# A float32 encoder on one core: feed-forward column groups projected in pairs, with seven products in place of eight in two block steps of each pair

## The chip, the cores and the metric

The kernel runs on one core of one Trainium2 chip. The metric is the device time of one execution in microseconds (us). Engines are named as in the profile: PE is TensorE (matmuls; PEld its weight loads), DVE is VectorE, ACT is ScalarE, POOL is GpSimd, SP is SyncE, which issues the weight loads from HBM.

## The reference

A trunk of two residual layers over 256 tokens of width 2048, in float32. The first layer mixes tokens by grouped-query attention, the second by a gated linear recurrence; each is followed by a SwiGLU feed-forward layer of inner width 5632, which is what the change touches:

```python
def swiglu(h, w_gate, w_up, w_down):
    return (jax.nn.silu(h @ w_gate) * (h @ w_up)) @ w_down

for i in range(DEPTH):
    h = rms_norm(x, norm_mix[i])
    ...
    x = x + mix
    x = x + swiglu(rms_norm(x, norm_ffn[i]), ffn_w_gate[i], ffn_w_up[i], ffn_w_down[i])
```

## The kernel before

**Numbers in two parts.** Each float32 operand is split into a rounded part `hi` and a rest `lo` (both float32r), and a product is made of three matmuls: hi x hi, hi x lo, lo x hi. Weights arrive as float32 in pieces of 512 KB, called halves here (`load_half`, L107): 128 rows by 8 x 128 numbers, in the feed-forward layers two tiles of contraction (k) by 512 columns. A load by SP fills `raw`, ScalarE casts it to `hi` (L116), VectorE makes `lo` = raw - hi (L117). Each of the three has five buffers, so a cast can begin when PE has left the half five places back.

**A projection with tokens in the rows.** `project_tokens` (L209) holds the activations' tiles as the stationary operand: 128 k by 128 tokens, for the two blocks a of the 256 tokens. It makes 512 columns at a time, in two PSUM banks, one for each token block. A half has 2 k x 2 token blocks x 3 = 12 matmuls of 512 columns.

**The feed-forward layer** (`ffn`, L634). The inner width of 44 tiles is done in three parts of 12, 16 and 16 tiles (`PARTS`). A part is made in units of 512 columns: first the gate (8 halves, 16 tiles of k), whose banks ScalarE turns into silu (`fg`), then up (8 halves), whose banks VectorE multiplies into `fu`. `turned` (L345) turns a unit so that the inner width lies on the partitions: VectorE transposes squares of 32 x 32 (`tb`), and 16 copies put them together (`tf`), every other one on ScalarE and on VectorE. The four tiles are then split into hi and lo (L645, L646). When a part is complete, `output` (L376) projects it down, four column groups of 512 one after the other, and adds each bank into the residual `x_tok` (L384). In the last part each finished column group is squared, turned and scaled for the next norm (`Norm.add`, L313; operands `xg`), while PE works on the next group. `PSUM` has two pools of four banks: `ps_a` for these projections, which take two each, and `ps_m`.

**What sets the order.** TensorE's instructions stand in the order in which the program issues them. The order of every other engine's queue is made by a scheduler at build time; on the chip each of them is worked off strictly in that order. Small pieces of work are hung on a counter of TensorE's steps (`later`, `step`). At the border between the two layers the recurrence begins with `project_two`, which takes the first 8 k tiles for two column tiles, then the other 8, and with `nr.spread`, four small matmuls that need the norm's factors.

Of the kernel before, what the change touches and what calls it, by code (L numbers as in the profile page):

```python
# [25 lines left out]
NBLK = 8  # L26
DFF = 5632
PARTS = [12, 16, 16]
HALF = 8
WIDE = 512  # L30
NCOL = D // WIDE
FOUR = WIDE // P
COMMON = {"sq", "nsq", "nr", "nrt", "rsq_s", "nj", "ndg", "nrb"}
EPS = 1e-6
LRU_C = 8.0
GRID_W = 64
# [33 lines left out]
def trunk(ctx, tc, w, out):  # L70
    nc = tc.nc
    act, dve, pool, pe, sync = nc.scalar, nc.vector, nc.gpsimd, nc.tensor, nc.sync
# [9 lines left out]
    ffn_scope = ctx.enter_context(ExitStack())  # L82
# [3 lines left out]
    def nm(s):  # L86
        uid[0] += 1
        return f"{s}_{uid[0]}"
# [14 lines left out]
        return i  # L103


    def load_half(src, n, pieces=1, then=None):
# [3 lines left out]
        newest["load"] = sync.dma_start(out=raw[:, :n, :], in_=src[:, :n, :])  # L110
        if then:
            then()
        for i in range(pieces):
            sl = slice(i * n // pieces, (i + 1) * n // pieces)
            newest["tiles"] = hi, lo
            newest["cast"] = act.copy(hi[:, sl, :], raw[:, sl, :])  # L116
            dve.tensor_tensor(lo[:, sl, :], raw[:, sl, :], hi[:, sl, :].bitcast(F32), ALU.subtract)  # L117
        return [(hi[:, i, :], lo[:, i, :]) for i in range(n)]
# [5 lines left out]
    def wide(name):  # L124
        src = w[name]
        return [(src[c, i], HALF) for c in range(src.shape[0]) for i in range(src.shape[1])]

    def ffn_order(l):
        units = [wide(f"w_gate{l}"), wide(f"w_up{l}")]
        seq, i = [], 0  # L130
        for p, n in enumerate(PARTS):
            for _ in range(n // FOUR):
                for u in units:
                    seq += u[i : i + KT // 2]
                i += KT // 2
            seq += wide(f"w_down{l}_{p}")
        return seq

    order = [(w["w_k"][i], HALF) for i in range(len(KEY_TILES))]
# [51 lines left out]
    def new_acc():  # L191
        return ps_a.tile([P, 2 * S], F32, tag="acc", name=nm("acc"))
# [18 lines left out]
    def project_tokens(xs, ready=0, close=None):  # L211
# [15 lines left out]
                step()  # L227
        return accs

    def three(o, hi, lo, x, start, stop):  # L230
        pe.matmul(o, hi, x[:, :S], start=start, stop=False)  # L231
        pe.matmul(o, hi, x[:, S:], start=False, stop=False)  # L232
        pe.matmul(o, lo, x[:, :S], start=False, stop=stop)  # L233
# [59 lines left out]


    class Norm:
        def __init__(self, gname, gofs):
            self.g = (gname, gofs)
            self.xs = []
            self.sums = tmp("nsq", (P, 2, NCOL))

# [12 lines left out]
        def add(self, c):  # L313
            for a in range(2):
                act.activation(tmp("nj", (P, WIDE), bufs=1), x_tok[:, a, c, :], AF.Square, accum_out=self.sums[:, a, c : c + 1])
            for f in turned(x_tok[:, :, c, :]):
                self.operand(f, True)


        def finish(self):  # L320
# [23 lines left out]
    def turned(src):  # L344
        b = fp[0].tile([P, 2, FOUR, P], F32, tag="tb", name=nm("tb"))  # L345
        f = fp[0].tile([P, 8, FOUR, 32], F32, tag="tf", name=nm("tf"))
        for a in range(2):
            dve.transpose(b[:, a, :, :], src[:, a, :])  # L348
        for q in range(4):
            for i in range(4):  # L350
                o, y = f[32 * i : 32 * i + 32, q::4, :, :], b[32 * q : 32 * q + 32, :, i, :]
                y = y.rearrange("p a (k t) -> p a k t", k=FOUR)
                if i % 2:
                    act.copy(o, y)  # L354
                else:
                    dve.tensor_copy(o, y)  # L356
# [19 lines left out]
    def output(xs, norm=None, end=False, ready=0, close=None):  # L376
        for c in range(NCOL):
            accs = project_tokens(xs, ready, None if c else close)
            for a, acc in enumerate(accs):
                n = 2 if end and c == NCOL - 1 else 1  # L380
                for i in range(n):
                    sl = slice(i * WIDE // n, (i + 1) * WIDE // n)
                    y = x_tok[:, a, c, sl]
                    dve.tensor_tensor(y, y, acc[:, sl], ALU.add)  # L384
                    if end:
                        sync.dma_start(out=out[:, a, c, sl], in_=y)
            if norm is not None:
                norm.add(c)
        if norm is not None:
            norm.finish()  # L390

# [8 lines left out]
    def table_act(*a, **k):  # L400
        table_op(act.activation(*a, **k))
# [226 lines left out]
        scope.pop()  # L628
        open_ffn()

    nf = Norm("norm_ffn", 0)
    output(o_t, nf, ready=KT - 2, close=end_attention)


    def ffn(norm, nxt):
        def unit():
            g, u = (fp[0].tile([P, 2, WIDE], F32, tag=t, name=nm(t), bufs=1) for t in ("fg", "fu"))
            for a, acc in enumerate(project_tokens(norm.xs)):
                table_act(g[:, a, :], acc, AF.Silu, scale=norm.rt[:, a : a + 1])
            for a, acc in enumerate(project_tokens(norm.xs)):  # L640
                dve.scalar_tensor_tensor(u[:, a, :], acc, norm.rt[:, a : a + 1], g[:, a, :], ALU.mult, ALU.mult)
            for f in turned(u):
                h = act_tile()
                hi, lo = (h[:, o : o + S].rearrange("p (q t) -> p q t", t=32) for o in (0, S))
                act.copy(hi, f)  # L645
                dve.tensor_tensor(lo, f, hi.bitcast(F32), ALU.subtract)  # L646
                yield h

        for p, n in enumerate(PARTS):
            hid = [h for _ in range(n // FOUR) for h in unit()]  # L650
            last = p == len(PARTS) - 1
            if last and nxt is not None:
                ln_exp_tables()
            output(hid, nxt if last else None, last and nxt is None)

    nr = Norm("norm_mix", KT)
    ffn(nf, nr)
# [127 lines left out]
        ln_exp_tables()  # L785
        open_ffn()

    nf = Norm("norm_ffn", KT)
    output(g_t, nf, ready=KT - 2, close=end_recurrence)
    ffn(nf, None)  # L790

# [84 lines left out]
```

## Time and profile before

| | |
|---|---|
| median of 3 runs | 2037.51 us (2037.05 to 2037.53) |
| span of the profiled execution | 2034.8 us |
| PE busy | 2021.0 us, 99% |
| DVE busy | 1311.9 us, 64% |
| ACT busy | 1157.2 us, 57% |
| read from HBM | 382.13 MB |

The span is that of one profiled execution, from the first to the last instruction; the runs' time has a little more around it. A busy engine is one with an instruction under way, and since PE's matmuls overlap, their rate is read from how many begin in a stretch, not from the length of one. In a row of a group of instructions the columns are: line, engine, operation, output<-inputs, shapes, count | busy us, mean ns of one | idle time of the engine just before them, and what ended it. In a window row: from:to, its length, busy time of PE, PEld, DVE, ACT and POOL with their counts, PE's granted clock, the share of DMA, GB/s; where PE alone was asked for, only its busy time and count stand ahead of the clock. In a timeline row: start, duration, engine, line, operation. In a row of waits: who waited for whom, us in total, times, the longest.

### The profile page before, as it was taken

How to read it: one execution, taken by the hardware profiler on the slowest of the kernel's cores; microseconds unless marked ns; L12 is line 12 of the kernel's file. 1: busy time of each engine (PE TensorE's matmuls, PEld its weight loads, DVE VectorE, ACT ScalarE, POOL GpSimd, SP SyncE). 2: the span in 40 equal slices, each digit the busy share in tenths (PEclk: the TensorE clock that was granted, in tenths of full speed). 3: DMA queues.
4: the chain of work that ended last, by engine and by line, in shares of the span. 5: the costliest groups of instructions: out<-in, count | busy, mean ns of one | idle time of the engine just before them, and what ended most of it. 6: DMA issues, size and time to landing. Idle time of an engine off the chain costs nothing.

```text
span 2034.8 us, 27445 instructions
## 1 busy us (share of the span) xinstructions
PE 2021.0 (99%) x10124; PEld 1722.5 (85%) x10124; DVE 1311.9 (64%) x1899; ACT 1157.2 (57%) x1776; POOL 168.6 (8%) x213
## 2 busy tenths in 40 slices
PE   9999999999999999999899999999999999999999
PEld 8898888888888888888799998888888888888887
DVE  7998765654665445667778987765555556555553
ACT  7665755544555345556689987755435554355442
POOL 1563000000000000000134330000000000000000
PEclk9999999999999999999999999999999999999999
DMA  8444565665666656666556555566666666666664
GB/s 319 157 135 145 186 202 193 186 203 191 187 197 197 195 195 193 186 199 196 188 165 188 187 157 194 180 205 197 190 194 195 193 190 196 196 189 195 197 202 129
DMA packets 108998, 386.02 MB, mean 190 GB/s; under 512 B 12224, under 2 KB 12992, under 8 KB 108736
## 3 DMA queue, kind: packets, MB, share of 16 engines
q1 hardware_dynamic: 108720, 384.26, 59.7%
q8 instruction: 79, 1.29, 0.3%
q14 instruction: 55, 0.45, 0.1%
q10 hardware_dynamic: 144, 0.02, 0.0%
HBM read 382.13 MB, written 2.10 MB: 189 GB/s over the span
## 4 chain that ended last, share of the span: by engine, by line
PE 54%; issue 40%; DVE 2%; DMA 2%; ACT 1%; POOL 0%; SPq 0%; DVEq 0%; POOLq 0%
PE acc L223 40%; PE acc L201 3%; PE acc L231 3%; PE acc L232 3%; PE acc L233 3%; PE pm L232 1%; PE pm L233 1%; PE pm L231 1%; DVE lo L117 1%; DMA x_tok<-in_xt_dram 1%; DMA graw<-in_w_gates_dram 0%; DMA raw<-in_w_k_dram 0%; PE pm L576 0%; DMA raw<-in_w_qv_dram 0%; ACT hi L116 0%
## 5 line engine op out<-in xcount | busy, mean ns | idle before, releaser
L117 DVE TENSOR_TENSOR lo<-raw,hi 128x1024 fp32r<-128x1024 f32 (+1 forms) x708 | 868.7, 1230 | 665.5 <-ACT hi L116 657.1
L116 ACT CAST hi<-raw 128x1024 fp32r<-128x1024 f32 (+1 forms) x708 | 739.4, 1047 | 751.7 <-PE acc L223 744.0
L223 PE MATMUL acc<-hi,xg 128*128 128x512 f32 x2816 | 867.8, 389 | 0.0
L223 PEld LDWEIGHTS acc<-hi,xg 128*128 128x128 f32 x2816 | 528.6, 188 | 109.6
L223 PE MATMUL acc<-hi,act 128*128 128x512 f32 x1920 | 594.2, 389 | 0.0
L223 PE MATMUL acc<-lo,xg 128*128 128x512 f32 x1408 | 547.7, 389 | 0.0
L223 PEld LDWEIGHTS acc<-hi,act 128*128 128x128 f32 x1920 | 360.4, 188 | 74.4
L223 PE MATMUL acc<-lo,act 128*128 128x512 f32 x960 | 373.5, 389 | 0.0
L223 PEld LDWEIGHTS acc<-lo,xg 128*128 128x128 f32 x1408 | 264.3, 188 | 54.9
L223 PEld LDWEIGHTS acc<-lo,act 128*128 128x128 f32 x960 | 180.2, 188 | 37.1
L231 PE MATMUL acc<-xg,hi 128*128 128x256 f32 x512 | 145.0, 283 | 0.0
L232 PE MATMUL acc<-xg,hi 128*128 128x256 f32 x512 | 145.0, 283 | 0.0
L233 PE MATMUL acc<-xg,lo 128*128 128x256 f32 x512 | 144.7, 283 | 0.0
L201 PE MATMUL acc<-xg,hi 128*128 128x512 f32 x384 | 125.8, 396 | 0.2 <-ACT hi L116 0.2
L354 ACT COPY tf<-tb 32x256 f32<-32x256 f32 x272 | 109.8, 404 | 3.7 <-DVE tb L348 0.2
L231 PEld LDWEIGHTS acc<-xg,hi 128*128 128x128 f32 x512 | 98.3, 192 | 0.0
L232 PEld LDWEIGHTS acc<-xg,hi 128*128 128x128 f32 x512 | 98.2, 192 | 0.1
L233 PEld LDWEIGHTS acc<-xg,lo 128*128 128x128 f32 x512 | 98.2, 192 | 0.0
L201 PEld LDWEIGHTS acc<-xg,lo 128*128 128x128 f32 x384 | 71.8, 188 | 16.0 <-DVE lo L117 1.9
L201 PE MATMUL acc<-xg,lo 128*128 128x256 f32 x384 | 84.8, 288 | 0.5 <-DVE lo L117 0.4
L356 DVE COPY tf<-tb 32x256 f32<-32x256 f32 x272 | 77.2, 284 | 4.0
L667 POOL MEMSET cb<- 128x2 f32 x16 | 1.7, 108 | 823.1 <-PE acc L233 811.6
(172 smaller groups left out, 1324.5 us busy)
## 6 DMA issues: line engine op xcount, KB each, us to landing
raw<-in_w_gate_dram SPq DMA_DIRECT2D x176, 512.0 KB, 4.0
raw<-in_w_up_dram SPq DMA_DIRECT2D x176, 512.0 KB, 3.9
raw<-in_w_down_dram SPq DMA_DIRECT2D x176, 512.0 KB, 3.8
raw<-in_w_in_dram SPq DMA_DIRECT2D x64, 512.0 KB, 4.3
raw<-in_w_qv_dram SPq DMA_DIRECT2D x40, 512.0 KB, 4.2
raw<-in_w_o_dram SPq DMA_DIRECT2D x32, 512.0 KB, 3.6
raw<-in_w_out_dram SPq DMA_DIRECT2D x32, 512.0 KB, 4.0
graw<-in_w_gates_dram SPq DMA_DIRECT2D x32, 256.0 KB, 3.4
```

What stands on the lines that cost most here:

```text
L116: newest["cast"] = act.copy(hi[:, sl, :], raw[:, sl, :])
L117: dve.tensor_tensor(lo[:, sl, :], raw[:, sl, :], hi[:, sl, :].bitcast(F32), ALU.subtract)
L201: pe.matmul(o, w, x, start=(k == 0 and not part), stop=(k == total - 1 and not part))
L223: pe.matmul(accs[a], x, wt[:, k, :], start=(k0 + k == 0 and n == 0), stop=(end and k == 1 and n == 2))
L231: pe.matmul(o, hi, x[:, :S], start=start, stop=False)
L232: pe.matmul(o, hi, x[:, S:], start=False, stop=False)
L233: pe.matmul(o, lo, x[:, :S], start=False, stop=stop)
L354: act.copy(o, y)
L356: dve.tensor_copy(o, y)
L667: pool.memset(b[:, 0:2], 0.0)
```

## The change

Two column groups are projected together (`project_pair`, new): gate and up of one unit, or two column groups of the down projection. A pair takes four PSUM banks (column group j, token block a), all of `ps_a`. In a normal step two tiles of k are taken for both groups: 2 halves, 8 products, 24 matmuls. In two steps of each pair (`SEVEN`: steps 1 and 3 of six, or 2 and 5 of eight) the 2 x 2 block product, tokens by k times k by columns, is made of seven products of block sums (Winograd's form): 21 matmuls. For those, VectorE and ScalarE make sums of weight blocks (`seven_forms`: four additions of 512 columns, one of them within the raw half, three of them into a tile `wx` of 1536 columns, which is cast to `wxh` and leaves a rest `wxl`) and sums of token blocks (`x_forms`, once for each operand and step, kept for all pairs). Four products go to banks of `ps_m`, and `merge` puts these together in `fg` and `fu`; they are then added to what comes from the four banks. The order of weight loads is interleaved to suit.

All 16 copies of `turned` go to ScalarE, and `tb` and `tf` have one buffer instead of two.

```diff
+SEVEN = {6: (1, 3), 8: (2, 5)}
...
+    def seven_forms():
+        load_half(*order[taken[0]])
+        r1, w1 = flat(newest["raw"]), [flat(t) for t in newest["tiles"]]
+        x, xh, xl = (fp[0].tile([P, 3, WIDE], t, tag=n, name=nm(n), bufs=1) for n, t in (("wx", F32), ("wxh", F32R), ("wxl", F32R)))
+
+        def sums(raw):
+            r2 = flat(raw)
+            dve.tensor_tensor(x[:, 0, :], r2[:, 0, :], r1[:, 0, :], ALU.add)
+            dve.tensor_tensor(r2[:, 0, :], r2[:, 0, :], r2[:, 1, :], ALU.add)
+            dve.tensor_tensor(x[:, 1, :], r2[:, 0, :], r1[:, 0, :], ALU.add)
+            dve.tensor_tensor(x[:, 2, :], x[:, 1, :], r1[:, 1, :], ALU.add)
+
+        load_half(*order[taken[0] + 1], before=sums)
+        w2 = [flat(t) for t in newest["tiles"]]
+        act.copy(xh, x)
+        dve.tensor_tensor(xl, x, xh[:].bitcast(F32), ALU.subtract)
...
+    def x_forms(h0, h1, tag):
+        y = fp[0].tile([P, 8, P], F32, tag="tb", name=nm("tb"))
+        for i, h in enumerate((h0, h1)):
+            o, hi, lo = y[:, 2 * i : 2 * i + 2, :].rearrange("p a t -> p (a t)"), h[:, :S].bitcast(F32), h[:, S:].bitcast(F32)
+            dve.tensor_tensor(o, hi, lo, ALU.add)
+        for o, a, b in ((4, 1, 3), (5, 0, 4), (6, 0, 1), (7, 2, 5)):
+            dve.tensor_tensor(y[:, o, :], y[:, a, :], y[:, b, :], ALU.subtract)
+        t = fp[0].tile([P, 2, 4, P], F32R, tag=tag, name=nm(tag), bufs=1)
+        act.copy(t[:, 0], y[:, 4:, :])
+        dve.tensor_tensor(t[:, 1], y[:, 4:, :], t[:, 0].bitcast(F32), ALU.subtract)
...
+    def project_pair(xs, forms, middle):
+        banks = [[new_acc() for _ in range(2)] for _ in range(2)]
...
+                product(p1, tokens(2 * n, 0), b11, last)
+                product(banks[0][0], tokens(2 * n + 1, 0), b21)
+                product(banks[1][0], s4, b22)
+                product(q7, s3, t3, last)
+                product(q5, s1, t1, last)
+                product(q6, s2, t2, last)
+                product(banks[0][1], tokens(2 * n + 1, 1), t4)
+                if last:
+                    middle(p1, q5, q6, q7)
+            else:
+                for j in range(2):
+                    half()
+                    hi, lo = (flat(t) for t in newest["tiles"])
+                    for a in range(2):
+                        for k in range(2):
+                            product(banks[j][a], tokens(2 * n + k, a), (hi[:, k, :], lo[:, k, :]), n == end and k == 1)
+        return banks
+
+    def merge(p1, q5, q6, q7):
+        g, u = (fp[0].tile([P, 2, WIDE], F32, tag=t, name=nm(t), bufs=1) for t in ("fg", "fu"))
+        act.copy(g[:, 0, :], p1)
+        dve.tensor_tensor(g[:, 1, :], q6, g[:, 0, :], ALU.subtract)
+        dve.tensor_tensor(u[:, 0, :], q5, g[:, 1, :], ALU.add)
+        dve.tensor_tensor(g[:, 1, :], q7, g[:, 1, :], ALU.subtract)
+        dve.tensor_tensor(u[:, 1, :], u[:, 0, :], q7, ALU.subtract)
+        return g, u
...
-                if i % 2:
-                    act.copy(o, y)
-                else:
-                    dve.tensor_copy(o, y)
+                act.copy(o, y)
...
-        fp[:] = [ffn_scope.enter_context(tc.tile_pool(name=nm("fp"), bufs=2))]
+        fp[:] = [ffn_scope.enter_context(tc.tile_pool(name=nm("fp"), bufs=1))]
...
+    def down(xs, forms, norm=None, end=False):
+        for c in (0, 2):
...
+            banks = project_pair(xs, forms, middle)
+            for j in range(2):
+                for a in range(2):
...
+                        dve.tensor_tensor(y, y, banks[j][a][:, sl], ALU.add)
...
+                if norm is not None:
+                    norm.add(c + j)
```

The scheduler's order changes with it. First pair: ScalarE at the border from the first layer's down projection to the recurrence (`raw`/`hi` are weight halves, `nj` the squares of a finished column group, `tf` its turned form, `xg` the operands). Before:

```order
L116 CAST hi_8768<-raw_8767 128x1024
L116 CAST hi_8876<-raw_8875 128x1024
L315 ACTIVATE nj_8630,nsq_3258<-x_tok 128x512
L315 ACTIVATE nj_8632,nsq_3258<-x_tok 128x512
L354 COPY tf_8635<-tb_8634 32x2x128 x8
L116 CAST hi_8906<-raw_8905 128x1024
L307 ACTIVATE xg_8654<-tf_8635,pk 128x256
```

Now, from the first cast of a half that is used behind the first four of the recurrence:

```order
L120 CAST hi_9393<-raw_9392 128x1024
L120 CAST hi_9423<-raw_9422 128x1024
L404 ACTIVATE nj_9111,nsq_3278<-x_tok 128x512
L404 ACTIVATE nj_9147,nsq_3278<-x_tok 128x512
L404 ACTIVATE nj_9149,nsq_3278<-x_tok 128x512
L120 CAST hi_9466<-raw_9465 128x1024
L445 COPY tf_9114<-tb_9113 32x2x128 x16
L515 ACTIVATE rsq_s_9187<-nrt_9183 128x2
L396 ACTIVATE xg_9133<-tf_9114,pk 128x256
...
L515 ACTIVATE nr_9186<-rsq_s_9187 128x2
L445 COPY tf_9152<-tb_9151 32x2x128 x16
L396 ACTIVATE xg_9171<-tf_9152,pk 128x256
```

Two column groups, with 16 copies each, now stand one behind the other after TensorE's last down matmul, with three weight casts between them and it; before there was one group with eight copies.

Second pair: ScalarE at the start of the first feed-forward layer, when the last column group of the attention's output is turned for the norm. Before:

```order
L315 ACTIVATE nj_3212,nsq_2358<-x_tok 128x512
L315 ACTIVATE nj_3214,nsq_2358<-x_tok 128x512
L354 COPY tf_3217<-tb_3216 32x2x128 x8
L116 CAST hi_3354<-raw_3353 128x1024
L307 ACTIVATE xg_3236<-tf_3217,pk 128x256
```

Now (`hi_3402` is the cast of the pair's seventh half, `wxh_3362` belongs to its first block step, the fifth and sixth half):

```order
L404 ACTIVATE nj_3232,nsq_2358<-x_tok 128x512
L404 ACTIVATE nj_3234,nsq_2358<-x_tok 128x512
L120 CAST hi_3365<-raw_3364 128x1024
L120 CAST hi_3402<-raw_3401 128x1024
L445 COPY tf_3237<-tb_3236 32x2x128 x16
L515 ACTIVATE rsq_s_3272<-nrt_3268 128x2
L252 CAST wxh_3362<-wx_3361 128x1536
L120 CAST hi_3420<-raw_3419 128x1024
```

The copies are twice as many, and they stand behind a weight cast further ahead and in front of the cast of the block sums.

Third pair: VectorE between the first and the second column groups of the first part's down projection. Before:

```order
L117 TENSOR_TENSOR lo_4419<-raw_4417,hi_4418 128x1024
L384 TENSOR_TENSOR x_tok<-x_tok,acc_4249 128x512
L384 TENSOR_TENSOR x_tok<-x_tok,acc_4250 128x512
L117 TENSOR_TENSOR lo_4437<-raw_4435,hi_4436 128x1024
```

Now, between the first pair of column groups and the second (`acc_4364` to `acc_4367` are the pair's banks in the order in which the next pair writes them):

```order
L121 TENSOR_TENSOR lo_4657<-raw_4655,hi_4656 128x1024
L498 TENSOR_TENSOR x_tok<-x_tok,acc_4364 128x512
L489 TENSOR_TENSOR x_tok<-x_tok,fg_4528 128x512
L489 TENSOR_TENSOR x_tok<-x_tok,fu_4529 128x512
L247 TENSOR_TENSOR wx_4661<-raw_4664,raw_4655 128x512
L498 TENSOR_TENSOR x_tok<-x_tok,acc_4366 128x512
L121 TENSOR_TENSOR lo_4666<-raw_4664,hi_4665 128x1024
L498 TENSOR_TENSOR x_tok<-x_tok,acc_4365 128x512
L121 TENSOR_TENSOR lo_4703<-raw_4701,hi_4702 128x1024
```

The adds that free the banks stand among the merge's adds, a block sum and weight rests, and the second bank's comes after the third's.

More of the change, by code (lines that the diff above doesn't have):

```diff
@@ L32 @@
 FOUR = WIDE // P
-COMMON = {"sq", "nsq", "nr", "nrt", "rsq_s", "nj", "ndg", "nrb"}
+COMMON = {"nsq", "nr", "nrt", "rsq_s", "nj", "ndg", "nrb"}
 EPS = 1e-6
@@ L132, in ffn_order @@
             for _ in range(n // FOUR):
-                for u in units:
-                    seq += u[i : i + KT // 2]
+                seq += sum(zip(*(u[i : i + KT // 2] for u in units)), ())
                 i += KT // 2
-            seq += wide(f"w_down{l}_{p}")
+            down = wide(f"w_down{l}_{p}")
+            for c in range(0, len(down), n):
+                seq += sum(zip(down[c : c + n // 2], down[c + n // 2 : c + n]), ())
         return seq
@@ L653, in ffn @@
                 ln_exp_tables()
-            output(hid, nxt if last else None, last and nxt is None)
+            down(hid, forms, nxt if last else None, last and nxt is None)
     nr = Norm("norm_mix", KT)
```

77 lines of the change are left out of this document (65 added, 12 removed).

## The prediction

> **What bounds the kernel now.** I read the page first (span, busy shares), then the groups of instructions kept apart by shape, then windows of busy time for the rate of TensorE, and last the timeline at the ends of stages.
>
> ```profile
> span 2034.8 us, 27445 instructions
> PE 2021.0 (99%) x10124; PEld 1722.5 (85%) x10124; DVE 1311.9 (64%) x1899; ACT 1157.2 (57%) x1776; POOL 168.6 (8%) x213
> L116 ACT CAST hi<-raw 128x1024 fp32r<-128x1024 f32 x702 | 736.9, 1052 | 751.0 <-PE acc L223 744.0 <-PE acc L201 4.3 <-DMA raw<-in_w_qv_dram 1.2
> L117 DVE TENSOR_TENSOR lo<-raw,hi 128x1024 fp32r<-128x1024 f32 x702 | 866.0, 1236 | 664.8 <-ACT hi L116 656.5 <-DMA graw<-in_w_gates_dram 6.5
> 300.00:400.00 100.00, 100.00 (x443) 82.81 (x442) 58.14 (x73) 50.27 (x65) 0.00 (x0) 1.00 0.61 193
> 293.00:960.00 667.00, 667.00 (x2945) 552.28 (x2944) 387.34 (x470) 332.64 (x431) 0.00 (x0) 1.00 0.62 194
> ```
>
> TensorE is idle for 13.8 us of the span in all (2034.8 - 2021.0) and never in the first feed-forward layer, 293 to 960 us: it is the bound. ScalarE's idle time before its casts ends on TensorE, VectorE's on ScalarE: both are ahead by the five weight buffers and wait for one to come free. 443 matmuls in 100 us are 0.2257 us each. A half (12 matmuls) takes 2.71 us, a product (3) 0.677, a step of two halves 5.42. VectorE is busy for 387 of 667 us (58%) there.
>
> **What the change removes.** A block step takes 21 matmuls, not 24, and each pair has two. There are 11 gate/up pairs and 6 pairs in the down projection of each layer, 34 in all: 34 x 2 x 3 = 204 matmuls, which is also what the row count of TensorE falls by. 204 x 0.2257 = 46.0 us, all of it on the bound.
>
> **What it adds.** The durations of the new operations come from the nearest shapes:
>
> ```profile
> L117 DVE TENSOR_TENSOR lo<-raw,hi 128x512 fp32r<-128x512 f32 x2 | 1.3, 690 | 0.6 <-ACT hi L116 0.6
> L384 DVE TENSOR_TENSOR x_tok<-x_tok,acc 128x512 f32<-128x512 f32 x62 | 39.6, 680 | 0.0
> L646 DVE TENSOR_TENSOR act<-tf,act 128x256 fp32r<-128x256 f32 x88 | 31.4, 419 | 0.0
> L330 DVE TENSOR_SCALAR ndg<-ident,nr 128x128 f32<-128x128 f32 x2 | 0.5, 282 | 0.0
> L641 DVE SCALAR_TENSOR_TENSOR fu<-acc,nr,fg 128x512 f32<-128x512 f32 x44 | 30.9, 744 | 0.0
> L348 DVE STREAM_TRANSPOSE tb<-fu 128x512 f32<-128x512 f32 x44 | 30.8, 701 | 0.0
> L356 DVE COPY tf<-tb 32x256 f32<-32x256 f32 x272 | 77.2, 284 | 4.0
> L354 ACT COPY tf<-tb 32x256 f32<-32x256 f32 x272 | 109.8, 404 | 3.7 <-DVE tb L348 0.2
> L116 ACT CAST hi<-raw 128x512 fp32r<-128x512 f32 x2 | 1.1, 618 | 0.5 <-DMA raw<-in_w_k_dram 0.5
> ```
>
> 128x1536 is not in the trace. From 512 to 1024 wide VectorE's row grows by 0.546 us, ScalarE's by 0.434, so I take 1.78 us for the block sums' rest and 1.49 for their cast; estimates, but 512 more columns can hardly cost less or twice as much.
>
> VectorE's queue in one gate/up pair: 16 rests x 1.236 = 19.8; two block steps x (4 x 0.69 + 1.78) = 9.1; merge of the four extra banks 4 x 0.68 = 2.7; adding the four banks 2.7; two products with the gate 1.5; transposes 1.4; rests of the hidden tiles 4 x 0.42 = 1.7: 38.9 us, and 2.66 more in the 16 places with token block sums (2 x 0.419 + 4 x 0.282 + 0.69). TensorE needs 186 x 0.2257 = 42.0 us for that pair. So VectorE goes from 61% of such a pair (the same rests, gate products, transposes and hidden rests with eight copies, 26.6 of 43.3 us) to 93%, at most 99%. A down pair of 16 tiles: 37.0 of 42.0 us; of 12 tiles: 32.1 of 31.1 us, over the bound.
>
> These sums are upper ones, since rows on VectorE overlap:
>
> ```profile
> 515.50 1.23 DVE L117 TENSOR_TENSOR lo<-raw,hi 128x1024 fp32r<-128x1024 f32 x1 [1.29 <-ACT hi L116]
> 516.65 1.43 DVE L646 TENSOR_TENSOR act<-tf,act 128x256 fp32r<-128x256 f32 x4
> ```
>
> A rest is followed after 1.15 us, not 1.23, and four of 0.419 take 1.43, not 1.68. I use 1.15, 0.60 for 512 columns and 0.35 for 256 where instructions stand back to back, which makes the fullest pair some 38 of 42 us. The Trainium skill, "VectorE: DVE Perf Modes", section "The DRAIN you can't avoid", says the next VectorE operation does not start until the pipeline is empty; by that the full sums of 99% and 103% would hold. The rows just shown start sooner, so the trace speaks against it here; it is one leg of the slower rival below.
>
> ScalarE takes over the 272 copies that VectorE made, 16 in a row instead of 8: 16 x 0.414 = 6.6 us (8 took 3.31, row below), during which no weight is cast. That, more than the sums, is what I expect to hurt. In a gate/up pair it is covered: counted from the pair's start, the eighth half is cast at 9.2 us (its buffer is left at 8.1), the copies end at 15.8, the ninth half is cast at 16.8 and split at 18.0, and TensorE reads it at 21.0. Three us are left; without that cover each of the 22 units would pay the 6.6 us less its lead. The banks of PSUM are all four in use, with no second set; in such a pair the first is read out 4 us before the next pair writes it, so this is nothing. Three places have no such cover.
>
> Place 1, start of each layer (second pair of orders above). The cast of the seventh half waits until TensorE has left the second, 5.4 us, and ends at 6.5; 16 copies to 13.1; the block sums' cast (wxh) to 14.8, their rest (wxl) to 16.5. TensorE gets to the second matmul of the first block-sum product after four halves and four products, 10.83 + 2.71 + 0.23 = 13.8 us: it waits 2.7, in two layers **5.4 us**.
>
> Place 2, first down part (12 tiles), where the block steps are the second and fourth of six. The copies stand behind the cast of the ninth half, whose buffer the first block step leaves at 8.1 us, and run from 10.2 to 16.8; one weight cast to 17.8, wxh to 19.3, wxl to 21.0; TensorE is there after two halves, a block step, two halves (5.42 + 4.74 + 5.42 = 15.6), four products and a matmul: 18.5. It waits 2.4 us. Then VectorE's row up to the add that frees the second bank (third pair of orders): 6 rests, 4 of 256, 14 of 512 columns = 6.9 + 1.4 + 8.4 = 16.7, so 37.7; TensorE wants that bank at 18.5 + 2.4 + 1.8 + 10.8 + 1.4 = 34.9 (the step's rest, four halves, two products) and waits 2.8. 5.2 a layer, **10.4 us**. Bounds for both places: 0 if ScalarE runs ahead, twice this if VectorE's rows don't overlap.
>
> Place 3, from the first feed-forward layer to the recurrent one.
>
> ```profile
> 986.96 0.62 ACT L315 ACTIVATE nj<-x_tok 128x512 f32<-128x512 f32 x1
> 988.45 3.31 ACT L354 COPY tf<-tb 32x256 f32<-32x256 f32 x8
> 992.74 1.71 ACT L307 ACTIVATE xg<-tf,pk 128x256 fp32r<-128x256 f32 x4
> 1000.79 0.37 ACT L338 COPY nrb<-pm 128x256 f32<-128x256 f32 x1
> PE pm L336 <- DVE ndg L330: 2.3, 1, 2.3
> PE pm L232 <- DVE xs L269: 2.2, 2, 1.3
> PE pm L231 <- ACT hi L116: 2.2, 1, 2.2
> 1003.77 0.28 PE L232 MATMUL acc<-xg,hi 128*128 128x256 f32 x1
> ...
> 1006.77 0.28 PE L233 MATMUL acc<-xg,lo 128*128 128x256 f32 x1
> ```
>
> Now only the last of four column groups comes late: TensorE has 72 matmuls of 0.12 us (25 steps of them in 3.00 us) = 8.6 us to do meanwhile, and waits 2.3 for the norm. The first projections are through 96 x 0.12 + 2.3 + 0.7 = 14.5 us after the last down matmul (T, about 986; 0.7 are the norm's own four matmuls and their hand-over). Changed, the last two groups come out together. ScalarE's queue from T (first pair of orders): two casts, held by buffers until T+3.9; squares T+6.3; one cast T+7.3; 16 copies T+13.9; four operands from T+14.5; 16 copies T+22.6; four operands T+24.3. TensorE has 48 matmuls, 5.8 us; waits 9.2, does 24, waits 5, and is through near T+27: 12.5 later than now. Its clock adds to that:
>
> ```profile
> 996.00:997.00 1.00, 0.00 (x0) 1.00 0.86 320
> 1009.00:1010.00 1.00, 0.36 (x1) 0.83 0.62 203
> 1010.00:1011.00 1.00, 0.06 (x1) 0.50 0.84 303
> 1016.00:1017.00 1.00, 1.00 (x9) 0.76 0.38 156
> ```
>
> The 2.3 us wait at 995 to 998 left the granted clock at 1.00; the nearly idle stretch from 1007 on brought it to 0.50 for some 7 us. A 9 us wait will too: 12 matmuls at half speed are 1.4 us more. Against that, the later wait of the gates for the convolution, with the slow clock behind it (2.2 + 2.2 us of waits, and half of 7), shrinks, since the norm's factors are then ready before TensorE is: I take 3 us back. Net **11 us**, bounds 6 and 16. The Trainium skill, "TensorE: Matmul & The Clock Gate", Part 1, puts the drop to half clock at an idle window of about 3.4 us; by it places 1 and 2, with waits under 3 us, mostly keep the clock, which is what the row at 996 shows.
>
> At the end the last two column groups leave together; their 0.5 us is little. DMA moves the same bytes in 3% less time: 194 GB/s becomes 200, nothing.
>
> **Sum.** 2034.8 - 46.0 + 5.4 + 10.4 + 11 + 0.5 = 2016.1 us of span. The median of the runs, 2037.51, lies 2.7 above the profiled span, so **2018.8 us**.
>
> **Rivals.** (a) Lookahead absorbs places 1 and 2: 2018.8 - 15.8 = 2003.0, less if place 3 costs 6: 1998. For it: TensorE waited nowhere in these layers with three or four halves ready. Against it: both waits are rows that stand in order on one queue, behind buffers that come free only with TensorE.
>
> (b) VectorE becomes the bound of the gate/up pairs, and the kernel slower. If its rows don't overlap (41.5 us) and it can't use its wait for ScalarE behind the 16 copies (by the count above it has nothing to do from 12.7 to 16.7 us, 4 us), a pair takes 45.5, not 42.0; half of that wait, in 22 units, 1.8 x 22 = 39 us on the forecast: 2058. It decides from (2037.5 - 2018.8) / 22 = 0.85 us a unit. For it: 93 to 99% by full durations, one queue that waits in order. Against it: the overlap shown, and that ScalarE can cast earlier once VectorE lags, since the buffers are then free.
>
> (c) The clock falls to half at each short wait: six waits x 7 us at half speed = 21 us more, 2040, no difference that can be told. Against it the row at 996.
>
> **How the numbers follow.** Forecast (waits at the three places only) 0.66, its own range 2008 to 2030; (a) 0.16; (b) 0.12; (c) 0.06. That the 204 matmuls do not go is no case, the built order shows them gone. A measurement of this kernel can tell 0.2%, 4 us. Faster: forecast, (a) and a sixth of (c), 0.83; same 0.06; slower 0.11. The range, 2000 to 2038, leaves out (b) and the lower half of (a).
>
> **What would show it.** L-rows of TensorE: 204 fewer matmuls at 0.2257 us. Its waits: two of about 2.7 us on wxl near the start of each layer, two of about 2.5 in each first down part, about 14 us for xg at the layers' border with the clock at 0.50 behind it, and none in the other 28 pairs. VectorE busy for about nine tenths of these layers. It would be wrong if TensorE waits for lo or wxl in most pairs (b), or only at the border (a).

## The result, and the profile after

The time did not change: 2037.48 us in the median of 12 runs (2032.23 to 2041.74) against 2037.21 (2036.19 to 2038.2) for the kernel before; ratio 0.9999, 95% interval 0.9991 to 1.0008. The forecast was 2018.8. The runs of the changed kernel lie 9.5 us apart from lowest to highest, those of the one before 2.0.

First the page of the changed kernel: span, busy shares, and the groups of the block sums.

```profile
span 2035.7 us, 27908 instructions
PE 1996.2 (98%) x9920; PEld 1689.5 (83%) x9920; DVE 1692.5 (83%) x2351; ACT 1369.3 (67%) x2166; POOL 168.7 (8%) x213
...
L245 DVE TENSOR_TENSOR wx<-raw,raw 128x512 f32<-128x512 f32 x68 | 47.0, 691 | 119.7 <-DMA raw<-in_w_up_dram 91.5
...
L253 DVE TENSOR_TENSOR wxl<-wx,wxh 128x1536 fp32r<-128x1536 f32 x68 | 119.1, 1752 | 22.4 <-ACT wxh L252 22.1
...
L252 ACT CAST wxh<-wx 128x1536 fp32r<-128x1536 f32 x68 | 100.3, 1476 | 34.5 <-DVE wx L248 34.5
```

TensorE has its 204 matmuls fewer (9920, not 10124), but is idle for 39.5 us (2035.7 - 1996.2) where it was idle for 13.8. The two new long rows last 1.75 and 1.48 us, as estimated (1.78, 1.49). The row to stop at is L245, the first addition of a block sum: it is busy for 47 us and VectorE stood idle ahead of it for 119.7, for a DMA.

The views of waits, TensorE's and then VectorE's own (who for whom, us in total, times, longest):

```profile
PE acc L319 <- ACT xg L396: 11.7, 2, 8.4
PE pm L275 <- ACT wxh L252: 6.3, 4, 2.0
PE pm L275 <- DVE wxl L253: 6.2, 5, 1.3
PE acc L275 <- DVE fg L755: 3.6, 6, 1.4
...
DVE wx L245 <- DMA raw<-in_w_up_dram: 91.5, 37, 4.0
DVE wx L245 <- DMA raw<-in_w_down_dram: 28.1, 15, 4.2
```

The first is the border; the next two are the places 1 and 2 of the prediction, but for one wait of 1.0 us at 965.71 in the last down pair of the first feed-forward layer. They make 24.2 us; what was given back is twice that. To find it, count matmuls in stretches instead of idle time. At the rate of the kernel before, in the window 293 to 960 shown ahead, one takes 667 / 2945 = 0.2265 us. Windows of the changed kernel:

```profile
274.00:300.00 26.00, 23.51 (x95) 18.72 (x95) 18.52 (x26) 19.29 (x33) 0.00 (x0) 0.93 0.55 183
...
412.00:440.00 28.00, 24.79 (x102) 19.64 (x101) 22.91 (x30) 17.46 (x29) 0.00 (x0) 0.94 0.48 153
440.00:970.00 530.00, 528.36 (x2319) 433.73 (x2318) 451.96 (x544) 339.01 (x468) 0.00 (x0) 1.00 0.60 198
...
1326.00:1350.00 24.00, 21.51 (x87) 17.07 (x86) 16.66 (x24) 17.56 (x31) 0.00 (x0) 0.93 0.57 191
...
1464.00:1490.00 26.00, 22.75 (x87) 17.97 (x86) 19.53 (x27) 15.73 (x28) 0.00 (x0) 0.87 0.50 161
1490.00:2030.00 540.00, 537.71 (x2363) 442.11 (x2362) 456.70 (x545) 320.35 (x419) 0.00 (x0) 1.00 0.59 194
```

The 95 matmuls of the first row need 21.5 us and got 26: 4.5 lost. In the same way place 1 of the second layer loses 4.3, place 2 4.9 and 6.3; together 20.0 us. The long stretches, in which TensorE is idle for only 1.6 and 2.3 us in all and the clock is at 1.00, lose 4.8 each (2319 x 0.2265 = 525.2 of 530), and 2.0 more go in the windows 300 to 412 and 1350 to 1464, which are not shown: 11.6. A matmul's row is 0.39 us long and the next begins after 0.226, so the first 0.16 us of a wait leave no idle time behind them, and the rows of waits miss them.

Where these 11.6 us lie can be read from the starts of TensorE's rows. In the four long stretches the gaps between two starts that are over 0.06 us too long add up to 10.8 us. Of these, 8.0 us in 13 pairs come 3.9 to 8.3 us after VectorE stood at L245 for a DMA, with no other stop of VectorE above 0.3 us in between. The largest, timeline of VectorE and TensorE:

```profile
1645.62 0.69 DVE L245 TENSOR_TENSOR wx<-raw,raw 128x512 f32<-128x512 f32 x1 [2.59 <-DMA raw<-in_w_up_dram]
...
1649.53 0.47 PE L275 MATMUL acc<-hi,xg 128*128 128x512 f32 x1 [1.36 <-DVE fg L755]
```

All six waits for `fg` in the rows of waits have such a stop 3.9 us ahead of them.

The third part is the stretch of the recurrence, from its first projection to the first matmul of the projection behind it. Timeline of TensorE, the kernel before, then the changed one:

```profile
985.80 0.28 PE L231 MATMUL acc<-xg,hi 128*128 128x256 f32 x1
...
1225.69 0.40 PE L223 MATMUL acc<-hi,act 128*128 128x512 f32 x1
```

```profile
978.58 0.28 PE L319 MATMUL acc<-xg,hi 128*128 128x256 f32 x1
...
1231.67 0.40 PE L228 MATMUL acc<-hi,act 128*128 128x512 f32 x1
```

239.9 us became 253.1: 13.2 more. The layers ahead of it and behind it (from 175.7 us, where the attention's output projection has just begun, to the first row; from the second row to the last matmul) went from 810.1 to 802.9 and from 804.9 to 799.8. Each should have lost 102 matmuls, 23.1 us, so they gave back 15.9 and 18.0. The account closes: 46.2 taken off, 15.9 + 13.2 + 18.0 = 47.1 given back, and the span is 0.9 longer. Below, "lost" for a layer is always this: its stretch less what its own count of matmuls asks for by the kernel before (787.0 and 781.8 us for all seven-product steps). For the first layer this is good to some 0.7 us: by that much it changes if the stretch is begun at the projection's own first row, which lies elsewhere in each kernel (174.6 us before, 174.3 now).

Now place 1 in the timeline:

```profile
274.38 6.65 ACT L445 COPY tf<-tb 32x256 f32<-32x256 f32 x16
...
281.16 1.46 ACT L252 CAST wxh<-wx 128x1536 fp32r<-128x1536 f32 x1
...
282.67 0.50 PE L275 MATMUL pm<-wxh,nf 128*128 128x512 f32 x1 [1.20 <-ACT wxh L252]
284.46 0.50 PE L275 MATMUL pm<-wxl,nf 128*128 128x512 f32 x1 [1.29 <-DVE wxl L253]
...
286.46 0.63 PE L275 MATMUL acc<-wxl,xg 128*128 128x512 f32 x1
286.88 0.63 PE L275 MATMUL acc<-wxh,xg 128*128 128x512 f32 x1
```

The chain is the forecast one: 16 copies, then the cast, then the rest, and TensorE waits 2.49 us for them with one matmul in between. But the last two rows are 0.42 us apart, not 0.226: half speed. The windows of 2 us (busy time and count of TensorE, then its granted clock) at place 1, and at place 2 of the second layer:

```profile
284.00:286.00 2.00, 1.54 (x5) 0.84 0.00 0
286.00:288.00 2.00, 2.00 (x6) 0.50 0.62 178
...
1474.00:1476.00 2.00, 2.00 (x5) 0.50 0.48 184
1476.00:1478.00 2.00, 2.00 (x6) 0.50 0.84 260
```

Over the whole span the mean granted clock fell from 0.998 to 0.992, which is 0.002 x 2034.8 = 4 us before and 0.008 x 2035.7 = 16 us now. At the four places 11.4 us are waits (2.49 twice, 3.20, 3.25) and the other 8.6 stand behind them, nearly all slow clock.

The border, timeline of ScalarE and TensorE:

```profile
985.61 6.60 ACT L445 COPY tf<-tb 32x256 f32<-32x256 f32 x16
...
992.89 0.58 PE L319 MATMUL acc<-xg,hi 128*128 128x256 f32 x1 [8.39 <-ACT xg L396]
...
1002.34 0.58 PE L319 MATMUL acc<-xg,hi 128*128 128x256 f32 x1 [3.26 <-ACT xg L396]
...
1013.72 0.28 PE L321 MATMUL acc<-xg,lo 128*128 128x256 f32 x1
...
1018.55 0.38 PE L319 MATMUL pm<-xs,ghi 128*128 128x256 f32 x1 [2.37 <-DVE xs L356]
```

Two waits, 8.4 and 3.3, each behind a run of 16 copies; the 150th matmul of the projections at 1013.72 (at 1006.77 before, where they began 7.2 later); and the gates still wait at 1018.

### The profile page after: what moved, and what is told of

The parts are those of the page before. It is cut to its first block, busy times and chain, and to the rows that moved or that the text cites. A ratio compares the mean times of both kernels' runs of the same rounds, so it can differ in the third digit from the quotient of the medians.

```text
span 2035.7 us, 27908 instructions
## 1 busy us (share of the span) xinstructions
PE 1996.2 (98%) x9920; PEld 1689.5 (83%) x9920; DVE 1692.5 (83%) x2351; ACT 1369.3 (67%) x2166; POOL 168.7 (8%) x213
## 4 chain that ended last, share of the span: by engine, by line
PE 47%; issue 42%; DVE 7%; DMA 2%; ACT 2%; POOL 0%; SPq 0%; DVEq 0%; ACTq 0%; POOLq 0%
PE acc L275 23%; PE acc L228 4%; PE acc L206 4%; PE pm L275 3%; DVE lo L121 3%; PE acc L319 3%; PE acc L320 3%; PE acc L321 3%; PE pm L320 1%; PE pm L321 1%; PE pm L319 1%; DMA raw<-in_w_up_dram 1%; ACT tf L445 1%; ACT hi L120 1%; DMA raw<-in_w_down_dram 0%
## 5 line engine op out<-in xcount | busy, mean ns | idle before, releaser
L275 PE MATMUL acc<-hi,xg 128*128 128x512 f32 x2200 | 697.7, 390 | 3.0 <-DVE fg L755 2.9
L275 PEld LDWEIGHTS acc<-hi,xg 128*128 128x128 f32 x2200 | 413.8, 188 | 95.5 <-issue 6.4
L275 PE MATMUL acc<-lo,xg 128*128 128x512 f32 x1100 | 428.6, 390 | 0.0
L275 PE MATMUL acc<-hi,act 128*128 128x512 f32 x1072 | 342.6, 391 | 0.9 <-DVE fg L755 0.7
L445 ACT COPY tf<-tb 32x256 f32<-32x256 f32 x544 | 219.5, 404 | 9.2 <-DVE xg L397 1.0
L275 PE MATMUL acc<-lo,act 128*128 128x512 f32 x536 | 209.2, 390 | 0.0
L228 PE MATMUL acc<-hi,act 128*128 128x512 f32 x512 | 159.9, 390 | 0.0
L245 DVE TENSOR_TENSOR wx<-raw,raw 128x512 f32<-128x512 f32 x68 | 47.0, 691 | 119.7 <-DMA raw<-in_w_up_dram 91.5
L321 PE MATMUL acc<-xg,lo 128*128 128x256 f32 x512 | 146.0, 285 | 0.0
L253 DVE TENSOR_TENSOR wxl<-wx,wxh 128x1536 fp32r<-128x1536 f32 x68 | 119.1, 1752 | 22.4 <-ACT wxh L252 22.1
L252 ACT CAST wxh<-wx 128x1536 fp32r<-128x1536 f32 x68 | 100.3, 1476 | 34.5 <-DVE wx L248 34.5
L275 PEld LDWEIGHTS acc<-lo,act 128*128 128x128 f32 x536 | 100.9, 188 | 20.4
```

Of the source, the lines that this page charges most:

```text
L228: pe.matmul(accs[a], x, wt[:, k, :], start=(k0 + k == 0 and n == 0), stop=(end and k == 1 and n == 2))
L245: dve.tensor_tensor(x[:, 0, :], r2[:, 0, :], r1[:, 0, :], ALU.add)
L252: act.copy(xh, x)
L253: dve.tensor_tensor(xl, x, xh[:].bitcast(F32), ALU.subtract)
L275: pe.matmul(acc, a, b, start=id(acc) not in begun, stop=last and i == 2)
```

## The experiments

Two theories were set against each other. The first: it is the places of the prediction, each wait about doubled by the clock, and all of them come from ScalarE's 16 copies. The second: VectorE is late in the pairs, be it by its load, as most of the expectations put it, or (six raw buffers, shared and six) because its in-order queue stops at the block sums until a weight half has landed. Each of the eleven kernels is the changed one with an edit whose main lines are shown, and each was timed against the kernel before on the same chip, which took 2036.7 to 2037.2 us.

| edit | median us | ratio to before, 95% | lost in layer 1 | recurrence | lost in layer 2 |
|---|---|---|---|---|---|
| none | 2037.48 | 0.9999 (0.9991 to 1.0008) | 15.9 | 253.1 | 18.0 |
| warm | 2031.0 | 0.9974 (0.9965 to 0.9983) | 14.6 | 251.2 | 14.5 |
| border unpaired | 2029.56 | 0.9964 (0.9952 to 0.9977) | 15.5 | 245.8 | 16.1 |
| first pairs' bad steps dropped | 2020.72 | 0.9922 (0.9909 to 0.9934) | 6.1 | 253.8 | 5.3 |
| pairs only | 2047.45 | 1.0051 (1.0038 to 1.0064) | 0.0 | 250.7 | 0.0 |
| border and drop | 2011.74 | 0.9879 (0.9866 to 0.9893) | 4.7 | 246.9 | 6.1 |
| six raw buffers | 2017.58 | 0.9908 (0.9895 to 0.9922) | 8.2 | 253.6 | 7.8 |
| copies shared | 2029.56 | 0.9969 (0.9957 to 0.998) | 16.7 | 244.9 | 16.8 |
| border, shared, six | 1999.41 | 0.9817 (0.9804 to 0.983) | 5.4 | 240.0 | 4.8 |
| order at place 1 | 2034.34 | 0.999 (0.9982 to 0.9999) | 16.5 | 253.8 | 13.3 |
| shared and six | 2004.1 | 0.9837 (0.9824 to 0.9851) | 4.5 | 245.1 | 4.6 |
| best | 1993.47 | 0.9788 (0.9775 to 0.9801) | 0.2 | 240.3 | 0.6 |

(Layers 1 and 2 here are the two feed-forward layers. For a kernel with more matmuls the 0.2265 us of each are counted in what it asks for; the warm kernel's added ones are not, they fill waits. The three columns on the right are of the one profiled execution, which lay within 1 us of the median but for three kernels: 2.3 us below it with the steps dropped, 2.6 above it with six raw buffers and with border, shared, six.)

**Warm: is it the clock?** At place 1, 10 matmuls with a tile of zeros stand ahead of the first block-sum product, at place 2, 12; they add nothing to the sum.

```diff
+                for _ in range(warm.get(n, 0)):
+                    pe.matmul(q5, zero, xs[0], start=id(q5) not in begun, stop=id(q5) not in begun)
```

> Edit: at the start of each feed-forward layer 10, and in the first down pair of each layer 12 matmuls of a zero tile are put ahead of the first block-sum product, so that TensorE is busy while it waits for the block sums (their result adds nothing). Theory A (the short waits at these four places bring the granted clock to half, and the slow stretch behind each costs as much as the wait): the waits of 2.5 and 3.2 us stay, now filled with work, the clock stays at 1.00 there, and the slow stretches go, about 2.5 + 2.5 + 2.7 + 4 = 11.7 us: 2026 (2023 to 2030). Theory B (VectorE, busy 83%, sets the pace, and the clock only follows): no gain, 2037 or a few us more for the added matmuls.

Windows of this kernel at place 1 and place 2:

```profile
284.00:286.00 2.00, 1.90 (x8) 1.00 0.00 0
...
422.00:424.00 2.00, 2.00 (x11) 1.00 0.36 133
```

The clock stays at 1.00 where it was 0.50, at all four places, and 6.5 us are gained, not the 11 or 12 expected. So slow clock is a real part of the loss at these places, but not all that stood behind the waits was to be had: in this kernel TensorE waits 2.4 us for the adds into `x_tok`, a wait that the changed kernel does not show. VectorE was the next one late.

**Border unpaired.** The last two column groups of layer 1 are projected one after the other again, without block sums (6 more matmuls).

```diff
+            if norm is not None and c:
+                return output(xs, norm, cols=(2, 3))
```

> Edit: in the last down part of the first layer only the first two column groups go as a pair, the other two one after the other as before the change, with 6 matmuls more (1.4 us). Theory A (the border between the layers loses 14.8 us more than before because two column groups come out together with 32 copies in a row on ScalarE): the wait of 8.4 and the one of 3.3 us for xg shrink to at most 3 in sum, the clock holds, 10 to 12 us less: 2026 (2024 to 2029). Theory B: the border's wait is one of VectorE's, which is no less busy: at most 4 us less, 2033 or more.

7.9 us gained, less than the 10 to 12 expected: 7.3 of them in the recurrence, 253.1 to 245.8, not all of the 13.2. One wait of 4.8 for `xg` is left, since the copies of one group are still 16 in a row on ScalarE.

**First pairs' bad steps dropped.** In each layer the early step of the first gate/up pair and the late step of the first down pair are made of eight products again: places 1 and 2 are gone, at the price of 12 matmuls.

```diff
-            banks = project_pair(xs, forms, middle)
+            banks = project_pair(xs, {1: forms[1]} if short and not c else forms, middle)
...
+            use = {5: norm.forms[5]} if first else norm.forms
```

> Edit: the first pair of each layer does its early block step with eight products, and the first down pair of each layer its late one; 4 of 68 steps, 12 matmuls more (2.7 us). Theory A (the loss in the layers stands at these four places, where the cast of the block sums stands behind 16 copies): waits and slow stretches there go, 5.0 + 5.0 + 5.2 + 7 = 22 us, less 2.7: 2018 (2014 to 2024). Theory B (VectorE's whole load): 4 of 68 steps are 6% of what was added, so 1 to 3 us less at most: 2034 to 2038.

Four of 68 block steps cost more than they bring: without them it is 16.8 us faster. The layers lose 6.1 and 5.3 now, a remainder in the other pairs for which the first theory has no place. The second in its form of load had asked for 2034 or more and fails here.

**Pairs only.** The pairs stay, with no block sums at all and (not shown) without the merge and its adds.

```diff
-SEVEN = {6: (1, 3), 8: (2, 5)}
+SEVEN = {6: (), 8: ()}
```

> Edit: pairs alone, every block step with eight products, no block sums, no merge; the copies stay on ScalarE. Theory A: the 46.0 us of matmuls come back, the waits in the layers go, the border's 14.8 us stay: 2037.2 + 14.8 = 2052 (2047 to 2055), with no PE wait inside the layers. Theory C (pairing itself, with all four PSUM banks in use, costs in every pair): beyond 2060, with PE waits at the pairs' ends.

TensorE's longest wait:

```profile
PE acc L319 <- ACT xg L396: 7.5, 2, 3.9
```

The layers take 810.1 and 804.9 us, what they took before. Pairing costs nothing there; all of its 10.7 us are at the border.

**Border and drop** together, to see whether the gains add:

> Edit: the border unpaired and the four early block steps left out, together. If the two losses are separate, their gains add: 2036.8 - 7.2 - 16.1 = 2013.5 (2010 to 2017).

They do: 7.9 + 16.8 off 2037.5 is 2012.8, measured 2011.74.

**Six raw buffers: the second theory.** A load then starts one half earlier, and the second half of a block step lies there when VectorE gets to L245.

```diff
-        raw = wp.tile([P, HALF, P], F32, tag="raw", name=nm("raw"), bufs=5)
+        raw = wp.tile([P, HALF, P], F32, tag="raw", name=nm("raw"), bufs=6)
```

> Edit: six raw buffers in place of five, so that the load of a half is issued one half earlier; VectorE waited 119.7 us in all for the second raw half of a block step, with its whole queue behind it. Theory A (those waits fall into VectorE's slack; what costs are the copies ahead of the block sums' cast): the 119.7 us shrink to a third or less, the four places stay, the time falls by at most 4 us: 2033 to 2038. Theory B (VectorE sets the pace): 34 pairs get 2 to 3.5 us of VectorE's time each, 10 us less or more: 2027 or lower.

Waits of VectorE:

```profile
DVE wx L245 <- DMA raw<-in_w_up_dram: 36.7, 37, 2.4
DVE wx L245 <- DMA raw<-in_w_down_dram: 23.0, 17, 3.0
```

Timeline of ScalarE at place 1:

```profile
272.28 1.48 ACT L252 CAST wxh<-wx 128x1536 fp32r<-128x1536 f32 x1
...
275.31 6.64 ACT L445 COPY tf<-tb 32x256 f32<-32x256 f32 x16 [0.59 <-DVE tb L440]
```

VectorE's waits for DMA are halved (119.7 to 59.7) and the kernel is 19.9 us faster, which the second theory had asked for. From 440 to 960 us TensorE does 2293 matmuls, where the changed kernel does 2280 and the kernel before 2296: the small losses are nearly gone. But the second fence says that two things were changed at once: the scheduler now puts the cast of the block sums ahead of the 16 copies, and place 1, with its 8.8 us, is gone. Place 2 is still there.

**Copies shared: the first theory.** Every other copy goes back to VectorE, as in the kernel before; five raw buffers.

```diff
-                act.copy(o, y)
+                if i % 2:
+                    act.copy(o, y)
+                else:
+                    dve.tensor_copy(o, y)
```

> Edit: every other one of the 16 copies back on VectorE, one buffer of each tile as in the changed kernel. Theory A (the 6.6 us in which ScalarE copies and casts nothing are the cause of the four waits and half of the border's chain): 3.3 us shorter copies end the waits of 2.5 and 3.2 us and take 6 to 7 us from the border: 22 + 7 = 29 us less, 2008 (2003 to 2016). Theory B (VectorE, which takes 77 us of copies on top of 1692, sets the pace): less than half of it, 2023 or more, with PE waits for lo and the added banks in most pairs.

Its waits of TensorE, and a window:

```profile
PE acc L275 <- DVE fg L758: 14.6, 12, 2.8
```

```profile
440.00:960.00 520.00, 515.59 (x2260) 422.77 (x2259) 460.13 (x611) 297.41 (x378) 0.00 (x0) 1.00 0.59 196
```

The border gets 8.2 better and the layers do not move: what the places no longer lose, TensorE loses in the pairs, 2260 matmuls in 520 us where 2296 would go, waiting for VectorE's adds into `fg`. VectorE is busy for 460 of 520 us there, and in the whole span still stands at L245 for 103 us. This is the second theory's number, and the first one's fell; the waits for `fg` are 12, though, and not in most pairs. Every one of them comes 5.0 us (one 7.3) after a stop of VectorE at L245 for a DMA, with VectorE at work all the time between. The longest, timeline of VectorE (the stop of TensorE that ends on this add is 2.84 us long and is shown in the last section):

```profile
1394.91 0.69 DVE L245 TENSOR_TENSOR wx<-raw,raw 128x512 f32<-128x512 f32 x1 [3.77 <-DMA raw<-in_w_up_dram]
...
1399.12 0.68 DVE L758 TENSOR_TENSOR fg<-acc,fg 128x512 f32<-128x512 f32 x1
```

**Border, shared, six** is all three at once:

> Edit: the copies shared again, the border unpaired, six raw buffers. Theory A: the border is nearly as before the change (at most 3 us more), the four places wait no longer, 6 matmuls fewer are saved: 2036.8 - 46.0 + 1.4 + 3 + 5 (short waits) = 2000 (1997 to 2006). Theory B: VectorE's load is the highest of all here, 2015 or more.

1999.41, as the first theory expected; VectorE's load, the highest so far, had stood for 2015 or more. The recurrence is back at 240.0. What is left in the layers is at place 2, the second bank's add of the prediction: 4.4 us in three waits for `x_tok`.

**Order at place 1**, to take the two effects of the six buffers apart: the copies of the first unit are put behind the cast of the block sums; five raw buffers.

```diff
+                if early and n == 2:
+                    for c in newest.pop("tf"):
+                        follow(c, newest["wxh"])
```

> Edit: at the start of each feed-forward layer the block sums' cast (wxh) is put ahead of the 16 copies on ScalarE, nothing else; five raw buffers, paired border, as changed. Theory A (place 1 is the order of these two entries, and the clock behind the wait costs about as much again): the waits of 2.5 us there are gone, 4.6 + 4.4 us less: 2028 (2025 to 2031). If only the waits count and the clock is nothing: 5 us, 2032. Theory B (VectorE sets the pace): no gain, 2036 or more.

Timeline of place 1:

```profile
280.87 0.39 PE L275 MATMUL pm<-wxh,nf 128*128 128x512 f32 x1
...
282.24 0.69 DVE L245 TENSOR_TENSOR wx<-raw,raw 128x512 f32<-128x512 f32 x1 [3.69 <-DMA raw<-in_w_up_dram]
```

The wait at place 1 is gone in both layers, with the drop of the clock (1.00 in all windows from 280 to 290), and 3.1 us are gained in place of 8.8, with runs that spread over 7.6 us here and 9.5 there. The second layer gains what place 1 had cost it (13.3 lost, 18.0 before); the first gains nothing (16.5 lost, 15.9 before). In the first layer VectorE, early now, stops at the next block sum for 3.69 us, its waits for DMA grow from 119.7 to 135.9, and those of TensorE for `fg` from 3.6 us in 6 to 6.5 in 11. The time lies between the two theories' numbers: the second layer did as the first theory says, the first layer as the second theory says. So with five buffers the order alone gives 3.1 of the 19.9 us; and a wait that is taken away can come back at another place as long as VectorE's queue stops for loads, as it did in one layer of two.

**Shared and six**, the second theory's sharpest number: the same shared copies that cost as much as they brought with five buffers.

> Edit: copies shared again and six raw buffers, the border paired. With the copies shared alone the layers lost 16.6 and 16.7 us of the 46. Theory B' (VectorE is so full that its waits for the second raw half, with the queue behind them, are no slack): with six buffers the layers lose 7 us each or less and the border 5: 2036.8 - 46.0 + 14 + 5 = 2010 (2004 to 2013). Theory A' (it is VectorE's instructions themselves that are too many with the copies back): little better than with the shared copies alone, 2020 or more.

A window, and VectorE's waits:

```profile
440.00:950.00 510.00, 509.85 (x2249) 421.74 (x2248) 460.03 (x606) 299.59 (x378) 0.00 (x0) 1.00 0.61 198
```

```profile
DVE wx L245 <- DMA raw<-in_w_up_dram: 20.7, 22, 1.7
```

25.5 us faster than with five buffers. VectorE has as much to do as there (460 us of this window, too), and the layers lose 4.5 and 4.6 in place of 16.7 and 16.8. It was not the amount of VectorE's work that kept TensorE waiting. The two sources differ in the buffer alone, but the scheduler's order differs too: some 140 of VectorE's 2623 instructions, about half of them of the block sums, stand at another place. So the times by themselves do not part the buffer from the order; that the waits followed the stops at L245 is what the trace of the five-buffer kernel shows, and with six buffers both are down, the stops from 103 to 33 us and the waits for `fg` from 14.6 us to none.

**Best**: border, shared copies, six buffers, and the late block step of each layer's first down pair made of eight products.

> Edit: six raw buffers, copies shared, border unpaired, and the first down pair of each layer with its early block step alone (6 matmuls more, 1.4 us). The one loss left in the layers, about 4 us each in that first down pair, where TensorE waits for the added bank, should go: 1999.4 - 8 + 1.4 = 1993 (1990 to 1998).

```profile
span 1992.6 us, 27905 instructions
PE 1979.7 (99%) x9932; PEld 1687.4 (85%) x9932; DVE 1747.6 (88%) x2595; ACT 1263.5 (63%) x1889; POOL 167.4 (8%) x213
```

1993.47 us, 2.1% faster than the kernel before (2036.74 beside it). It has 192 matmuls fewer, 43.5 us, and is 43.3 faster: the block products pay in full once nothing is given back.

## Why the prediction was wrong

**The number of matmuls: right.** 204, and they still go at 0.2265 us where nothing waits.

**"None in the other 28 pairs": the step that failed first.** VectorE was taken to be late only if its rows did not fit into a pair, and they do: it is busy for 443 of 520 us from 440 to 960, 85%, no more than the overlapping rows said. Its idle time was counted as free. But L245 stands on its queue before the second half of the block step has landed, and everything behind it, rests for TensorE too, stands still with it: 119.7 us in 52 waits. That leaves almost no slack in some pairs, and the pairs other than those at the places lose 11.6 us, 13.9 with the 2.3 that the account finds outside these windows. The prediction's sum has no term for them. It is what rival (b) named, a queue that waits in order, by another wait and at 0.4 us a pair in the mean (13.9 / 34). That this wait makes the larger part of the loss is shown by the traces, 8.0 us of it gap by gap, and borne out by the two kernels with shared copies, in which the layers' loss falls from 16.7 and 16.8 us to 4.5 and 4.6 with the stops. What makes the other 5.9 us was not taken apart; 1.0 of it is the wait at 965.71. The kernel before was not run with six buffers; it loses nothing in its layers, so there is little to gain there. The Trainium skill, "VectorE: DVE Perf Modes", section "The DRAIN you can't avoid", on which the prediction drew for rival (b), adds that a next operation that is not held starts earlier; so the overlapping rows need not speak against it.

**"Short waits keep the clock": the second.** It rested on one wait of 2.3 us. The waits of 2.5 and 3.2 us with a single matmul inside brought the clock to 0.50 at all four places. Rival (c) had the time right (2040), the mechanism in half: six drops would have cost 21 us by it, the clock's share is about 8.6 at the places and, by the mean clock, some 12 in all.

**Places 1 and 2: cause and wait right, price too small.** 2.49 us of wait against 2.7 at place 1, 3.2 against 2.4 for the first wait of place 2; lost 8.8 against 5.4, and 11.2 against 10.4. Place 2 comes out near only by chance: the second bank's wait of 2.8 did not come, the slow clock came. That wait is real: it shows at 1.8 us each as soon as TensorE gets there sooner (six buffers: 3.8 us in 3 for `x_tok`).

**The border: right, but for what it gives back.** TensorE waited 8.4 and 3.3 (forecast 9.2 and 5). The 150th matmul of the projections began at 985.8 + 21.0 before and begins at 978.6 + 35.1 now, 14.1 later against 12.5 + 1.4. The 3 us to come back at the gates did not: TensorE still stopped there, for `xs`, and lost the clock again. 14.1 less 0.9 is 13.2, against 11; within the bounds of 6 and 16.

By the same sum, with these terms: 2034.8 - 46.2 + 8.8 + 11.2 + 13.2 + 13.9 = 2035.7, the span measured. That the measured time lies inside the range of 2000 to 2038, at its end, is luck: the range was drawn for other losses than the largest one here.

## What to carry to other kernels

Before calling an engine's idle time slack, see what stands at the head of its queue while it idles: in an in-order queue a wait for a load delays all that is behind it, and one more buffer can be worth more than moving work to another engine. A short stop of TensorE should be priced at up to twice its length: here 11.4 us of stops cost 20.0. And a saving spread over many steps is best kept where it has cover: here four of 68 steps (20.0 us) and the border (13.2) ate more than half of the 46.2.

## What the runs showed of the hardware

A stop's length alone does not tell whether the clock falls. With shared copies (five buffers) a stop of 2.84 us kept it, with six buffers one of 1.82 us lost it. Timeline and window of the one, then of the other:

```profile
1399.94 0.47 PE L275 MATMUL acc<-hi,xg 128*128 128x512 f32 x1 [2.84 <-DVE fg L758]
```

```profile
1400.00:1402.00 2.00, 2.00 (x9) 1.00 0.69 248
```

```profile
1476.82 0.73 PE L275 MATMUL acc<-hi,act 128*128 128x512 f32 x1 [1.82 <-DVE x_tok L498]
```

```profile
1478.00:1480.00 2.00, 2.00 (x6) 0.50 0.83 270
```

The same wait of 1.82 us in the other layer of that kernel (at 432.59) kept the clock at 1.00. The Trainium skill, "TensorE: Matmul & The Clock Gate", Part 1, says that the clock is set by a free-running window of about 3.4 us, so that it depends on where in it an event falls. That agrees with like stops having unlike effects, and would make the spread of the changed kernel's runs (9.5 us, against 2.0) no surprise; that this is the spread's cause was not shown, but the mean clock goes with it: 0.990 in the slowest run, 0.991 to 0.993 in the six fastest, and 0.002 of 2036 us is 4 us. The Trainium skill also says there that an idle window is what slows the clock. A stop of 1.82 us fills no such window, and the clock fell: here the measurement decides, and a part-idle window can be enough.
